# A row maximum over 16384 rows: two stores at the end, a last row in halves, and six rows per partition reduced by TensorE, ScalarE and GpSimd

## The chip, the cores and the metric

The kernel runs on one core of one Trainium2 chip. The metric is the device time of one execution in microseconds (us), given as the median of several runs. Beside the runs there is one execution that the hardware profiler recorded; its durations are the ones used in the working.

## What is computed

```python
def setup_inputs():
    batch, seq, dim = 32, 512, 1024
    return {"x": np.random.randn(batch, seq, dim).astype(np.float32)}

def reference(x):
    return np.max(x, axis=-1).astype(np.float32)
```

The input is 32 x 512 = 16384 rows of 1024 floats (67.1 MB); the output is one float for each row (64 KB). Every input value is read once, so the loads alone are a large part of the time.

## The kernel before

The 16384 rows are cut into two blocks. In a block of S rows per partition, partition p holds S rows that follow one another in memory, so that a load of g rows per partition moves one run of g x 4 KB for each of the 128 partitions. The first block has 112 rows per partition, the second 16. "Row" below always means one row in each of the 128 partitions.

`BLOCKS` (L13 to L16) lists how many rows each load brings: large loads first (14, 14, 12, ...), then smaller ones down to single rows at the end. There are 26 loads. They go into `ring` (L37), a buffer of 46 rows; a load that doesn't fit behind the last one starts again at place 0 (L46, L47), and has to wait until VectorE has reduced the rows that stood there.

For each load there are two statements: SyncE's queue issues the load (L49), and VectorE reduces it to one value a row with one `reduce_max` (L50), which writes into `res`. After each block, ScalarE's queue issues the store of that block's part of `res` (L54). TensorE, ScalarE's arithmetic and GpSimd do nothing, but for four small memsets of the launch (L71).

What sets the order: each engine and each queue takes its instructions in the order of the program. The framework adds the waits: a reduction waits for its load, a load for the reductions that last read its places, a store for the block's reductions. The framework also shares out a few semaphores among all transfers of the SyncE and ScalarE queues in turn, so that a transfer can have to wait for an earlier one to land. L82 is the end of the program.

Of the kernel before, what the change touches and what calls it, by code (L numbers as in the profile page):

```python
# [1 line left out]

# [4 lines left out]


F32 = mybir.dt.float32

BLOCKS = [  # L13
    [14, 14, 12, 11, 9, 8, 8, 7, 6, 5, 4, 4, 4, 3, 3],
    [2, 2, 2, 2, 2, 1, 1, 1, 1, 1, 1],
]  # L16
RING = 46


@with_exitstack  # L20
def kernel(
    ctx: ExitStack,
    tc: tile.TileContext,
    x: bass.AP,
    out: bass.AP,
):
    nc = tc.nc
    P = 128
    X = mybir.AxisListType.X

    xf = x.flatten_outer_dims()
    N, D = xf.shape
    I = N // P
    of = out.flatten_outer_dims()

    once = ctx.enter_context(tc.tile_pool(name="once", bufs=1))
    ring = once.tile([P, RING, D], F32)  # L37
    res = once.tile([P, I], F32)

    at = first = 0  # L40
    for loads in BLOCKS:
        S = sum(loads)
        xb = xf[first * P:(first + S) * P, :].rearrange("(p i) d -> p i d", p=P)
        b = 0
        for g in loads:
            if at + g > RING:  # L46
                at = 0  # L47
            xc = ring[:, at:at + g, :]
            nc.sync.dma_start(out=xc, in_=xb[:, b:b + g, :])  # L49
            nc.vector.reduce_max(out=res[:, first + b:first + b + g], in_=xc, axis=X)  # L50
            at += g
            b += g
        dst = bass.AP(tensor=of.tensor, offset=of.offset + first * P, ap=[[S, P], [1, S]])
        nc.scalar.dma_start(out=dst, in_=res[:, first:first + S])  # L54
        first += S
    assert first == I


# [1 line left out]
_INS = ['x']  # L60
_OUTS = [((32, 512), 'float32')]


# [23 lines left out]
```

## Time and profile before

| | us |
|---|---|
| median of 10 runs | 165.1 (164.98 to 165.37) |
| the profiled execution | 165.25 |
| its span, first to last instruction | 163.5 |
| VectorE busy, 26 reductions | 138.5 |
| VectorE idle, waiting for loads (4 times) | 22.5, of which 20.3 for the first load |
| first load issued | 0.73 |
| first store (56 KB): issued, time to landing | 143.04, 6.6 |
| last reduction: start, duration | 159.82, 1.21 |
| last store (8 KB): issued, time to landing | 161.07, 1.4 |

The profiled execution took 165.25 us, of which 163.5 lie between the first and the last instruction. Times within the profile count from the start of that span. "DVE" in the profile is VectorE, "POOL" is GpSimd, "SPq" is SyncE's queue, "ACTq" ScalarE's. In the row of 40 digits each digit is the busy share of a fortieth of the span in tenths. In the groups of instructions, the columns are: how many, busy time in all, mean nanoseconds of one, idle time before them and what ended it. The chain of waits is followed back from the last instruction: at each step the profile goes to whatever released it last.

### The profile page before, as it was taken

To read this page: it belongs to the slowest core of one execution; us is meant where nothing else is said; L and a number is where in the kernel's file an instruction comes from. 1 tells how busy PE (TensorE), PEld (TensorE's weight loads), DVE (VectorE), ACT (ScalarE), POOL (GpSimd) and SP (SyncE) were. 2 spreads that over 40 slices of the span, in tenths; PEclk is the share of its full clock that TensorE was granted. 3 is DMA by queue.
4 is the path that set the end of the run, shared out by engine and by line. 5 is a ranking of instruction groups with operands and counts; after the bars stand their busy time and mean duration, and the time that the engine had idled before them with its cause. 6 is when DMAs were issued, how large, how long until landed. Compare 5 with 4: busy or idle time off the path is not lost.

```text
span 163.5 us, 109 instructions
## 1 busy us (share of the span) xinstructions
DVE 138.5 (85%) x26; POOL 0.2 (0%) x4
## 2 busy tenths in 40 slices
DVE  0000099968999999999999999999999999999994
POOL 0000000000000000000000000000000000000000
DMA  6999999999899898999999999999999999999980
GB/s 225 449 449 449 449 449 449 449 405 397 385 433 497 353 518 350 433 433 455 441 401 473 409 442 414 427 415 446 410 425 433 429 414 420 419 420 419 411 342 2
DMA packets 4032, 67.18 MB, mean 411 GB/s; under 512 B 704, under 2 KB 704, under 8 KB 1472
## 3 DMA queue, kind: packets, MB, share of 16 engines
q1 hardware_dynamic: 3744, 67.11, 96.3%
q10 hardware_dynamic: 288, 0.07, 0.2%
HBM read 67.11 MB, written 0.07 MB: 411 GB/s over the span
## 4 chain that ended last, share of the span: by engine, by line
DMA 57%; DVE 40%; DVEq 1%; SPq 0%; issue 0%
DMA ring<-in_x_dram 57%; DVE res L50 40%; DVEq L82 1%; SPq L49 0%
## 5 line engine op out<-in xcount | busy, mean ns | idle before, releaser
L50 DVE TENSOR_REDUCE res<-ring 128x1 f32<-128x1024 f32 (+11 forms) x26 | 138.5, 5396 | 22.5 <-DMA ring<-in_x_dram 22.5
L71 POOL MEMSET const-bfloat16-1.0<- 128x1 bf16 x1 | 0.1, 101 | 0.0
L71 POOL MEMSET const-uint8-127<- 128x1 uint8 x1 | 0.1, 101 | 0.0
L71 POOL MEMSET const-float32-0.0<- 128x1 f32 x1 | 0.1, 98 | 0.2 <-issue 0.2
L71 POOL MEMSET const-float32-1.0<- 128x1 f32 x1 | 0.1, 98 | 0.0
## 6 DMA issues: line engine op xcount, KB each, us to landing
ring<-in_x_dram SPq DMA_DIRECT2D x2, 7168.0 KB, 27.8
ring<-in_x_dram SPq DMA_DIRECT2D x2, 4096.0 KB, 31.6
ring<-in_x_dram SPq DMA_DIRECT2D x1, 6144.0 KB, 50.1
ring<-in_x_dram SPq DMA_DIRECT2D x3, 2048.0 KB, 36.7
ring<-in_x_dram SPq DMA_DIRECT2D x1, 5632.0 KB, 29.6
ring<-in_x_dram SPq DMA_DIRECT2D x5, 1024.0 KB, 24.6
ring<-in_x_dram SPq DMA_DIRECT2D x1, 4608.0 KB, 23.6
ring<-in_x_dram SPq DMA_DIRECT2D x1, 3584.0 KB, 38.3
```

What stands on the lines that cost most here:

```text
L50: nc.vector.reduce_max(out=res[:, first + b:first + b + g], in_=xc, axis=X)
L71: nc = _bacc.Bacc("TRN2", target_bir_lowering=False, num_devices=1)
L82: with _tile.TileContext(nc) as tc:
```

## The change

It has three parts that stand in one diff.

First, the stores. Both are issued after all loads. The first block's store gets a dependency of its own on the last reduction of the loop, so that it can't go out earlier.

Second, the last row. Its 1024 values are loaded in two halves. The first half goes to a place in the ring, the second into a small buffer `tail` with 16 places ahead of it. VectorE writes the first half's maximum into the place just ahead of the second half, and then reduces this place and the second half together, which gives the row's maximum.

Third, six rows. Each entry of `BLOCKS` is now (rows loaded, rows of these that VectorE does not reduce, number of the load after whose reduction their results are taken in; loads count from 0). Loads 7 and 9 give away two rows each, loads 10 and 12 one each. Such a row goes through four engines: TensorE turns it in eight pieces of 128x128 into PSUM, so that the 128 partitions lie along the free axis; ScalarE copies the 128x1024 result back; GpSimd takes the maximum over partitions (`partition_all_reduce`); TensorE turns the result back, in eight pieces of one partition, which gives eight partial maxima for each row in PSUM; and VectorE takes the maximum of these eight. `in_turn` ties the instructions of TensorE, and those of VectorE, into the order in which the program names them. A row's turn back is held in a list (`backs`) and put into the program behind the next given-away row's `partition_all_reduce`, or at the next load that gives none away. The identity that TensorE needs is made by GpSimd after the first load has landed.

The load lists change as well: 20 loads in the loop and two halves, in place of 26.

```diff
 BLOCKS = [
-    [14, 14, 12, 11, 9, 8, 8, 7, 6, 5, 4, 4, 4, 3, 3],
-    [2, 2, 2, 2, 2, 1, 1, 1, 1, 1, 1],
+    [(15, 0, -1), (15, 0, -1), (15, 0, -1), (15, 0, -1), (12, 0, -1), (7, 0, -1), (11, 0, -1), (10, 2, 8), (7, 0, -1), (5, 2, 13)],
+    [(4, 1, 15), (2, 0, -1), (2, 1, 18), (1, 0, -1), (1, 0, -1), (1, 0, -1), (1, 0, -1), (1, 0, -1), (1, 0, -1), (1, 0, -1)],
 ]
 RING = 46
...
+    turn = ctx.enter_context(tc.tile_pool(name="turn", bufs=2))
+    allr = ctx.enter_context(tc.tile_pool(name="allr", bufs=2))
+    psum = ctx.enter_context(tc.tile_pool(name="psum", bufs=3, space=bass.MemoryType.PSUM))
+    psmall = ctx.enter_context(tc.tile_pool(name="psmall", bufs=2, space=bass.MemoryType.PSUM))
...
+    PAD = 16
+    tail = once.tile([P, PAD + H], F32)
...
+    def in_turn(engine, inst):
+        if engine in before:
+            tc.add_manual_dep(inst.ins, before[engine].ins.name, NOSYNC, reason="in turn")
+        before[engine] = inst
+        return inst
+
+    def by_gpsimd(rows, cols, m):
+        back = psmall.tile([P, m, C], F32)
+        for k in range(m):
+            ps = psum.tile([P, D], F32)
+            for c in range(C):
+                in_turn("PE", nc.tensor.transpose(
+                    out=ps[:, c * P:(c + 1) * P],
+                    in_=rows[:, k, c * P:(c + 1) * P],
+                    identity=ident,
+                ))
+            sb = turn.tile([P, D], F32)
+            nc.scalar.copy(out=sb, in_=ps)
+            top = allr.tile([P, D], F32)
+            nc.gpsimd.partition_all_reduce(top, sb, P, bass_isa.ReduceOp.max)
+            run(backs)
+
+            def turn_back(top=top, k=k):
+                for c in range(C):
+                    in_turn("PE", nc.tensor.transpose(
+                        out=back[:, k, c:c + 1],
+                        in_=top[0:1, c * P:(c + 1) * P],
+                        identity=ident[0:1, 0:1],
+                    ))
+
+            backs.append(turn_back)
+        return lambda: in_turn("DVE", nc.vector.reduce_max(out=cols, in_=back, axis=X))
+
+    def run(calls):
+        while calls:
+            calls.pop(0)()
...
-            xc = ring[:, at:at + g, :]
-            nc.sync.dma_start(out=xc, in_=xb[:, b:b + g, :])
-            nc.vector.reduce_max(out=res[:, first + b:first + b + g], in_=xc, axis=X)
...
-        nc.scalar.dma_start(out=dst, in_=res[:, first:first + S])
+            xc = ring[:, at:at + n, :]
+            nc.sync.dma_start(out=xc, in_=xb[:, b:b + n, :])
+            cols = res[:, first + b:first + b + n]
+            if m:
+                due.setdefault(w, []).append(by_gpsimd(xc[:, n - m:, :], cols[:, n - m:], m))
+            else:
+                run(backs)
+            if j == 0:
+                nc.gpsimd.tensor_copy(out=ident[:, 0:1], in_=xc[:, 0, 0:1])
+                make_identity(nc, ident)
+            if n > m:
+                reduce = in_turn("DVE", nc.vector.reduce_max(
+                    out=cols[:, :n - m], in_=xc[:, :n - m, :], axis=X))
+            run(due.get(j, []))
...
+    half = ring[:, at, :H]
+    nc.sync.dma_start(out=half, in_=xb[:, b, :H])
+    nc.sync.dma_start(out=tail[:, PAD:], in_=xb[:, b, H:])
+    in_turn("DVE", nc.vector.reduce_max(out=tail[:, PAD - 1:PAD], in_=half, axis=X))
+    in_turn("DVE", nc.vector.reduce_max(out=res[:, I - 1:], in_=tail[:, PAD - 1:], axis=X))
+
+    store = nc.scalar.dma_start(out=views[0][0], in_=views[0][1])
+    tc.add_manual_dep(store.ins, reduce.ins.name, SYNC, reason="behind the loads")
+    nc.scalar.dma_start(out=views[1][0], in_=views[1][1])
```

In it D = 1024, H = D // 2 = 512, C = D // 128 = 8, P = 128, and `ident` is a 128x128 identity; `views` keeps each block's destination and its part of `res`.

## The prediction

> **What bounds the kernel now.** I read the page's busy shares first, then the chain of waits in order of time, then the waits of the load queue, then the groups by shape, then narrow windows at the end.
>
> ```profile
> span 163.5 us, 109 instructions
> DVE 138.5 (85%) x26; POOL 0.2 (0%) x4
> DMA  6999999999899898999999999999999999999980
> ```
>
> The transfers are busy in every slice but the last, and VectorE in 85% of the span. Neither can be called the bound from shares alone: the chain has to say which one is late where.
>
> ```profile
> 1.15 36.06 DMA ring<-in_x_dram
> 37.23 58.01 DVE res L50 x5
> 95.26 36.75 DMA ring<-in_x_dram
> 132.03 19.94 DMA ring<-in_x_dram
> 151.99 7.92 DVE res L50 x6
> 159.91 1.13 DVEq L82
> ```
>
> (Start, duration.) The two alternate. At 95.26 and 151.97 VectorE had caught up and was waiting for a load; in between and after, it was working without a pause. From 151.99 it reduces 8 rows (seven instructions, the timeline gives 9.04) without a wait and ends at 161.03.
>
> ```profile
> SPq L49 <- DVE res L50: 77.6, 7, 15.1
> SPq L49 <- DMA ring<-in_x_dram: 56.6, 10, 18.2
> SPq L49 <- DMA out_dram<-res: 5.0, 1, 5.0
> ```
>
> (Total, times, longest.) The load queue waits a lot, but only for room: the transfers stay busy beneath it. The third line is the first block's store: issued at 143.04, landed 6.6 later at 149.64, and one load of the tail was issued only then (149.7). The loads issued before it were still landing until 157.0, so this wait cost no transfer time.
>
> Issue time plus time to landing gives each load's landing. 14 rows land at 20.3 and 37.2; 12 at 51.8; 11 at 65.0; the last 3-row load at 139.4; the last of the five two-row loads at 151.97; the six singles at about 1.27 apart until 159.6. An n-row load therefore costs about 1.20n + 0.08 (14 rows: 16.9; 4 rows: 4.9; 1 row: 1.27). Checked over the whole: 20.3 + 114 x 1.20 + 25 x 0.08 = 159.1, plus some 0.3 for the store (its queue's 0.2% of the span): 159.4, measured 159.6. So **the loads set the pace**, and VectorE adds a last row and 0.2 of lag behind them.
>
> ```profile
> L50 DVE TENSOR_REDUCE res<-ring 128x14 f32<-128x14336 f32 x2 | 30.2, 15086 | 22.1 <-DMA ring<-in_x_dram 22.1
> L50 DVE TENSOR_REDUCE res<-ring 128x2 f32<-128x2048 f32 x5 | 11.2, 2280 | 0.2 <-DMA ring<-in_x_dram 0.2
> L50 DVE TENSOR_REDUCE res<-ring 128x1 f32<-128x1024 f32 x6 | 6.8, 1208 | 0.0
> ```
>
> The mean ns give VectorE's price: (15086 - 1208) / 13 = 1.068 us a row and about 0.14 an instruction, of which 0.07 shows between instructions that follow directly (9.04 = 8 x 1.068 + 7 x 0.07). VectorE's row is 0.13 cheaper than the loads'; it catches up slowly.
>
> [...]
>
> **The change, part by part.** Loads are numbered 1 to 20 in the new lists, then two halves.
>
> *Store moved.* The first block's store goes from the middle of the tail to behind load 20's reduction. It takes its 0.3 of transfer time out of the load stream, and its queue wait with it. It is put on ScalarE's queue ahead of the last store; issued at about 158.8, 0.38 on the queue, its 56 KB then lands beside the last half row and before the last store is even issued (160.1). Cost 0; if it should land as slowly as before (6.6), the end would be 165.4 instead of 161.5, but that landing was with eight loads queued ahead, which are gone here.
>
> *Load lists.* 22 loads for 26: 4 x 0.08 = 0.3 less. First load 15 rows: 20.3 + 1.2 = 21.5. Then 113 rows x 1.20 + 21 x 0.08: the last half lands at 158.8 (was 159.6). Room in the ring: load 4 needs reduction 1 (21.5 + 16.15 = 37.7) while loads 2 and 3 are queued until 57.7; load 5 needs reduction 2 (55.8), load 6 and 7 reduction 3 (74), loads 8 to 11 reductions 4 and 5 (92, 105), all with more than 15 us of loads ahead of them. Cost 0. GpSimd's rows never gate a load: their places are not used again.
>
> *VectorE.* Load 4 lands at 75.8, and VectorE needs 45 rows until load 8: 75.8 + 48.1 + 4 x 0.07 = 124.1, which is just load 8's landing (124.1). From there it has 32 rows (six fewer than landed), 15 instructions and four small maxima over 8 or 16 values out of PSUM: 34.2 + 1.1 + 4 x 0.15 + 0.1 for the last = 36.0, ending at **160.1**. The small maxima are not in the trace; 0.14 is VectorE's fixed part[...]. The halves: two instructions of 0.61 for one of 1.14; the second can start at 159.4, after its landing at 158.8, so VectorE, not the load, is last, by some 0.7. Without the six rows (6 x 1.07 = 6.4) it would end at 166.5: they are what makes the rest possible.
>
> *The six rows.* For each: eight TensorE transposes F, ScalarE's copy c, GpSimd's maximum A, eight turns back B. None is in the trace.
> [...]
>
> Round trip F + c + A + B = 6.2. TensorE's order is written out by hand, and a row's turn back stands ahead of a later row's transposes: row 5's transposes stand behind row 3's turn back, row 6's behind row 5's. So from load 10's landing (138.65) to row 6's result there are **three whole round trips**, 18.6: 157.2. VectorE reaches the maximum that needs it (after load 19) at 157.5. It fits with 0.3 to spare. The earlier ones: rows 1 and 2 from 124.1 to 133[...], needed at 140.3; row 4 at 148, needed at 151.5; row 5 at 151, needed at 153.9. Behind a late maximum on VectorE stand load 20, both halves and both stores, so lateness goes straight into the end, threefold.
>
> *Setup.* The identity is made on GpSimd after load 1, at 21.5 with 100 us before use: 0. If it delayed the first load instead, all of its time would be seen.
>
> *Sum.* VectorE ends 160.1 for 161.03: -0.9. The store and closing stay 2.45 (163.5 - 161.03). Profiled execution: 165.25 (span 163.5 and 1.75 around it) -> 164.3. The median of the runs, 165.1, lies 0.15 under it: **164.2**.
>
> **Rivals.**
> - *The gain is eaten* (same): load 8 lands 0.4 later, as the measured excess of 0.2 and single-row spacing of up to 1.4 allow, and the small maxima take 0.25 with their waits: 160.1 + 0.4 + 0.4 = 160.9, so 165.0. For it: VectorE is the later of the two over the whole last 36 us, with no wait left to swallow anything. Against: the loads are fewer.
> - *The round trip is too long* (slower): its place is VectorE's wait for row 6, after load 19. It decides from 3 x (round trip) > 18.85 + 0.9 + 0.3, a round trip of 6.7. At 7.5 row 6 comes at 161.15, 3.65 late, and the time is 164.15 + 3.65 = 167.8.[...] For it: only 0.5 separates my estimate from it, and four terms are unseen. Against: no profile row[...].
>
> **How the numbers follow.** A difference of 0.2% (0.33 us) is about what a measurement of this kernel can tell from none. Forecast 0.57 (own range 163.6 to 164.7), eaten 0.10, too long 0.33. About half of the last lies below 167.8 (a round trip of 7.5). The range 163.6 to 167.8 leaves out the rest of it, some 0.17, and 0.02 below.
>
> **What would show it.** Right: VectorE's busy time near 134 (122 x 1.068 + 22 x 0.14 + 0.6); no wait of VectorE for TensorE over 0.3; the last load landing near 158.8; VectorE's end near 160.1. GpSimd's mean of one near 2.9 and the eight transposes within 1.4. Wrong: VectorE waiting for TensorE after load 19 (too long), a late first store, or POOL work ahead of the first load.

## The result and the profile after

| | before | after |
|---|---|---|
| median of the runs, us | 165.11 (28 runs) | 169.09 (8 runs, 168.29 to 170.21) |
| profiled execution | 165.25 | 168.57 |
| its span | 163.5 | 166.6 |
| time around the span | 1.75 | 1.97 |
| VectorE's last reduction ends | 161.03 | 164.32 |

The changed kernel is slower: ratio 1.0241, 95% interval 1.0224 to 1.0258. The forecast was 164.2 and faster. The rival "the round trip is too long" had the sign and the place; its own number, 167.8, was still 1.3 short.

As in the prediction, loads are counted from 1 here. Of the six rows that VectorE gives away, 1 and 2 come with load 8, 3 and 4 with load 10, 5 with load 11 and 6 with load 13.

The page of the changed kernel, in the order in which the kernel before was read: busy shares, then the shares of the chain.

```profile
span 166.6 us, 329 instructions
PE 16.5 (10%) x96; PEld 14.7 (9%) x96; DVE 132.7 (80%) x26; ACT 7.4 (4%) x7; POOL 20.2 (12%) x13
DMA 56%; DVE 29%; POOL 4%; PE 4%; issue 3%; POOLq 2%; ACT 1%; SPq 0%; ACTq 0%
```

VectorE does 5.8 us less than before, as the six rows promise, and none of the new engines is busy for more than 12%. Shares of busy time would call this a good trade. But POOL, PE and ACT have appeared in the chain. Who waited for whom (total, times, longest):

```profile
DVE res L124 <- DMA ring<-in_x_dram: 28.0, 5, 21.3
DVE res L95 <- PE back L88: 3.5, 1, 3.5
POOL ident masks.py:199 <- issue: 10.0, 1, 10.0
```

L95 is VectorE's maximum over the turned-back values, L88 the turn back. One wait of 3.5 us, where I had worked out 0.3 to spare; the 10.0 of GpSimd comes back below. The chain of waits of the changed kernel shows what it waited for (start, duration, what):

```profile
139.46 1.99 PE ps L75 x8
...
141.53 1.02 ACT sb L81
142.55 0.08 issue
142.63 3.23 POOL top L83
145.86 0.04 issue
145.91 1.01 PE back L88 x8
146.92 1.92 PE ps L75 x8
...
150.01 3.22 POOL top L83
153.24 4.11 issue
157.34 3.28 POOLq L168
160.63 0.04 issue
160.67 1.02 PE back L88 x8
161.69 0.02 issue
161.71 0.04 DVE res L95
161.75 0.04 issue
161.80 1.21 DVE res L124
163.01 0.60 DVE tail L136
163.61 0.02 issue
163.63 0.69 DVE res L137
```

Read it from the top: load 10 has landed; turn, copy, maximum and turn back of row 3; then the turn of row 5 right behind that turn back at 146.92; and so on. The "issue" of 4.11 hides row 5's turn back and row 6's turn and copy, and "POOLq L168" is row 6's maximum. The timeline of TensorE has the turns in full, with row 5's turn back just ahead of row 6's transposes.

```profile
145.91 1.01 PE L88 MATMUL back<-ident,top 1*128 1x1 f32 x8 [3.13 <-POOL top L83]
146.85 1.97 PE L75 MATMUL ps<-ident,ring 128*128 128x128 f32 x8
149.12 1.01 PE L88 MATMUL back<-ident,top 1*128 1x1 f32 x8 [0.30 <-POOL top L83]
153.29 1.01 PE L88 MATMUL back<-ident,top 1*128 1x1 f32 x8 [3.17 <-POOL top L83]
154.23 1.97 PE L75 MATMUL ps<-ident,ring 128*128 128x128 f32 x8
160.67 1.01 PE L88 MATMUL back<-ident,top 1*128 1x1 f32 x8 [4.47 <-POOL top L83]
```

Row 6's data landed at 149.3, and TensorE was free between 150.13 and 153.29. It stood still for 3.17 us in front of row 5's turn back, which waited for GpSimd, while the transposes behind it were ready. From 139.46 to 161.69 there are three round trips of 7.4: 22.2 us instead of the 18.6 of the prediction.

The second difference lies much earlier. Load 8 landed at 124.8 instead of 124.1, because load 2 came 18.6 us after load 1, where 18.1 had been worked out. VectorE, which has no slack from there on, asks for row 6 at 158.2 instead of 157.5.

### The profile page after: what moved, and what is told of

Its sections match the earlier page's. It is cut to its first block, busy times and chain, and to the rows that moved or that the text cites. A ratio compares the mean times of both kernels' runs of the same rounds, so it can differ in the third digit from the quotient of the medians.

```text
span 166.6 us, 329 instructions
## 1 busy us (share of the span) xinstructions
PE 16.5 (10%) x96; PEld 14.7 (9%) x96; DVE 132.7 (80%) x26; ACT 7.4 (4%) x7; POOL 20.2 (12%) x13
## 3 DMA queue, kind: packets, MB, share of 16 engines
q1 hardware_dynamic: 3168, 67.11, 94.4%
HBM read 67.11 MB, written 0.07 MB: 403 GB/s over the span
## 4 chain that ended last, share of the span: by engine, by line
DMA 56%; DVE 29%; POOL 4%; PE 4%; issue 3%; POOLq 2%; ACT 1%; SPq 0%; ACTq 0%
DMA ring<-in_x_dram 56%; DVE res L124 28%; POOL top L83 4%; PE ps L75 2%; POOLq L168 2%; ACT sb L81 1%; PE back L88 1%; DVE res L137 0%; DVE tail L136 0%; SPq L113 0%; DVE res L95 0%; ACTq L81 0%
## 5 line engine op out<-in xcount | busy, mean ns | idle before, releaser
L124 DVE TENSOR_REDUCE res<-ring 128x1 f32<-128x1024 f32 (+7 forms) x20 | 131.3, 6600 | 28.1 <-DMA ring<-in_x_dram 28.0
L83 POOL PARTITION_ALL_REDUCE top<-sb x6 | 19.4, 3256 | 109.2 <-ACT sb L81 109.2
L75 PE MATMUL ps<-ident,ring 128*128 128x128 f32 x48 | 10.9, 415 | 128.8 <-DMA ring<-in_x_dram 128.8
L75 PEld LDWEIGHTS ps<-ident,ring 128*128 128x128 f32 x48 | 9.5, 222 | 128.9 <-issue 124.9
L81 ACT COPY sb<-ps 128x1024 f32<-128x1024 f32 x6 | 6.1, 1012 | 149.2 <-PE ps L75 149.2
L88 PE MATMUL back<-ident,top 1*128 1x1 f32 x48 | 5.7, 235 | 16.4 <-POOL top L83 16.4
L88 PEld LDWEIGHTS back<-ident,top 1*128 1x128 f32 x48 | 5.2, 201 | 18.0 <-POOL top L83 18.0
L95 DVE TENSOR_REDUCE res<-back 128x2 f32<-128x16 f32 (+1 forms) x4 | 0.7, 162 | 3.5 <-PE back L88 3.5
L137 DVE TENSOR_REDUCE res<-tail 128x1 f32<-128x513 f32 x1 | 0.7, 687 | 0.0
L136 DVE TENSOR_REDUCE tail<-ring 128x1 f32<-128x512 f32 x1 | 0.7, 676 | 0.0
## 6 DMA issues: line engine op xcount, KB each, us to landing
ring<-in_x_dram SPq DMA_DIRECT2D x1, 5120.0 KB, 32.3
```

What stands on the lines that cost most here:

```text
L75: in_turn("PE", nc.tensor.transpose(out=ps[:, c * P:(c + 1) * P], in_=rows[:, k, c * P:(c + 1) * P], identity=ident,))
L81: nc.scalar.copy(out=sb, in_=ps)
L83: nc.gpsimd.partition_all_reduce(top, sb, P, bass_isa.ReduceOp.max)
L88: in_turn("PE", nc.tensor.transpose(out=back[:, k, c:c + 1], in_=top[0:1, c * P:(c + 1) * P], identity=ident[0:1, 0:1],))
L95: return lambda: in_turn("DVE", nc.vector.reduce_max(out=cols, in_=back, axis=X))
L124: reduce = in_turn("DVE", nc.vector.reduce_max(out=cols[:, :n - m], in_=xc[:, :n - m, :], axis=X))
```

## The experiments

Two theories stand after this. **Round trips:** three of them in a row, tied together by TensorE's written order, each longer than estimated, put row 6 late. **Late loads:** something around 20 to 40 us delays load 2, in some executions load 3 as well, by 0.4 to 1.2 us together, and the whole kernel with them. Rivals of the first: GpSimd's four maxima in a row are the limit; the use of GpSimd costs time by itself. Rival of the second: longer loads are slower.

### The first step of the change alone

Edit: the load lists of before, no row given away; both stores at the end, last row in halves.

> The load lists of before (the last single row in two halves), both stores at the end, no row given away. If the loss of the change sits only in the six rows, as the round-trip theory says, this part alone should be a little faster than before: the store's 0.3 us leaves the load stream (last landing 159.3 for 159.6) and the last reduction shrinks from 1.21 to about 0.7, so 0.5 to 0.8 us faster, 164.3 to 164.6. If the stores' move or the halves cost something, it is at or over 165.1.

Measured: 165.24 against 165.09, ratio 1.0009 (1.0001 to 1.0017). The promised 0.5 to 0.8 isn't there; the kernel is 0.15 slower, and the interval only just leaves out no difference. In the end of its chain the two halves run directly behind the singles:

```profile
151.72 7.74 DVE res L120 x6
159.46 0.10 issue
159.56 0.69 DVE tail L132
160.25 0.02 issue
160.27 0.69 DVE res L133
```

VectorE, not the load, is last. A last load in halves can't help there: it makes two instructions (0.69 + 0.69 and the small waits) out of one of 1.21. To tell the halves from the store, the store was moved alone (`held` is the last reduction but one; the diff is against the kernel before):

```diff
-        nc.scalar.dma_start(out=dst, in_=res[:, first:first + S])   # behind each block
+    store = nc.scalar.dma_start(out=views[0][0], in_=views[0][1])   # behind all loads
+    tc.add_manual_dep(store.ins, held.ins.name, SYNC, reason="behind the loads")
```

> The kernel before with nothing changed but the first block's store, which now waits for the last reduction but one. The prediction had it take 0.3 us out of the load stream: 164.8. e1_stores_halves (165.2, with the halves) saw a last landing only 0.1 to 0.2 earlier, so the other reading is: the 56 KB cost the loads 0.1 at most, and with the last row whole, 164.9 to 165.1.

Measured: 165.00 against 165.11, ratio 0.9992 (0.9986 to 0.9998). The last load landed 139.2 us after the first (159.2 and 20.0; before: 139.3). The store had cost the loads 0.1, not 0.3; its landing took only 1.6 us at the end. So the store gives 0.1 and the halves take 0.2 to 0.3 in this setting.

### TensorE's order: one turn back later

```diff
             else:
-                run(backs)
+            elif j != 11:
+                run(backs)
```

(`j` counts from 0, so this is load 12 by the counting of the text.) Load 12 no longer puts row 5's turn back into the program; it comes behind row 6's transposes.

> The changed kernel with one line different: the turn back of row 5 stays behind row 6's transposes on TensorE. Round-trip theory: row 6's transposes then start at about 150.1 instead of 154.2, GpSimd takes rows 5 and 6 back to back (153.2 to 156.5), row 6's result is there at 157.6, before VectorE asks for it at 158.2; the 3.5 us wait is gone and VectorE ends near 160.8, so 3.5 us faster than the changed kernel: about 165.0 by the profile beside it. If GpSimd's own time is the limit, or if the loss lies outside the wait, it stays above 167.

Measured: 165.83 (ratio 1.0046, 1.0027 to 1.0065), 3.3 us under the changed kernel. VectorE has no wait for TensorE left. GpSimd takes rows 5 and 6 0.55 apart (lines of the timeline of this kernel):

```profile
149.94 3.22 POOL L83 PARTITION_ALL_REDUCE top<-sb  x1 [0.39 <-ACT sb L81]
153.71 3.22 POOL L83 PARTITION_ALL_REDUCE top<-sb  x1 [0.55 <-ACT sb L81]
156.99 1.01 PE L88 MATMUL back<-ident,top 1*128 1x1 f32 x8 [2.77 <-POOL top L83]
158.64 0.15 DVE L95 TENSOR_REDUCE res<-back 128x1 f32<-128x8 f32 x1
```

Row 6 is back at 158.0, before VectorE asks for it at 158.64. GpSimd itself was not the limit. The time isn't 165.0 but 165.8, though VectorE's end, 161.30, is near the 160.8 expected: the late loads were 0.5 later still here, and the time around the span was 2.4 in this execution.

### Two rows fewer

```diff
-    [(4, 1, 15), (2, 0, -1), (2, 1, 18), (1, 0, -1), ...
+    [(4, 0, -1), (2, 0, -1), (2, 0, -1), (1, 0, -1), ...
```

> The changed kernel with rows 5 and 6 given back to VectorE (four rows through GpSimd, none after load 9). Round-trip theory: the wait is gone, VectorE has 2 x 1.07 us more and two small maxima of 0.15 less: it ends at 164.3 - 3.5 + 2.1 - 0.3 = 162.6, so about 1.7 us faster than the changed kernel and 1.8 slower than before (166.9). If using GpSimd at all costs time outside VectorE's path, the distance between VectorE's end and the device time is larger than the 4.2 us of before.

Measured: 166.88 (1.011, 1.0096 to 1.0125); VectorE ends at 162.57, 162.6 expected, without a wait for TensorE. The distance from VectorE's end to the device time is 166.62 - 162.57 = 4.05 (before: 4.22), so no hidden price of using GpSimd shows here. Giving the two rows back costs VectorE 2 us of work and still beats the changed kernel by 2.2.

### How many round trips count

```diff
+            mid = once.tile([P, D], F32)
-            nc.scalar.copy(out=sb, in_=ps)
+            nc.scalar.copy(out=mid, in_=ps)
+            nc.scalar.copy(out=sb, in_=mid)
```

The changed kernel, with each row's copy made in two steps.

> The changed kernel with ScalarE's copy made twice (PSUM to a buffer, buffer to the GpSimd input), which adds 1.0 to 1.2 us to each row's round trip and nothing to TensorE or GpSimd. Theory of three round trips in a row: row 6 comes 3 x 1.1 = 3.3 us later, 172.4. If GpSimd's four maxima in a row set row 6 (two round trips and four maxima), 2.2 us later, 171.3. If only row 6's own latency counts, 1.1 us, 170.2.

Measured: 172.23 (1.0438, 1.0418 to 1.0459), 3.1 over the changed kernel. In the profile, row 6's maximum on GpSimd and then on VectorE:

```profile
161.21 3.22 POOL L85 PARTITION_ALL_REDUCE top<-sb  x1 [5.29 <-ACT sb L83]
165.54 0.17 DVE L97 TENSOR_REDUCE res<-back 128x1 f32<-128x8 f32 x1 [4.97 <-PE back L90]
```

VectorE's part starts 3.83 later than in the changed kernel (161.71); 0.43 of this is load 10, whose transposes start at 139.89 for 139.46. The rest, 3.40, is three times 1.13: the second copy's 1.04 and its handover. Two trips (2.3) or one (1.1) are excluded. The prediction's "threefold" holds.

### Does GpSimd cost time by itself?

```diff
+            if first == 0 and b == 0:
+                nc.gpsimd.tensor_copy(out=src, in_=xc[:, 0, :])
+                nc.gpsimd.partition_all_reduce(top, src, P, bass_isa.ReduceOp.max)
```

> The kernel before with one GpSimd copy and one partition maximum of 128x1024 behind the first load, whose result nobody uses (the output is that of before). It is off every path, so the round-trip theory expects 165.1 plus nothing. The rival[...] expects 0.2 to 1 us more, either as a later landing of the loads around 20 to 40 us (in the changed kernel load 2 came 18.6 us after load 1, where 18.1 was worked out) or outside the span (time less span was 1.75 before and 2.0 to 2.9 in the runs of the changed kernel).

Measured: 165.22 against 165.09 (1.0006, 0.9998 to 1.0014): nothing that can be told from none. Then the same with an identity made as in the change:

```diff
+                make_identity(nc, ident)
```

> The kernel before with the same idle GpSimd work as e4_one_maximum and the making of an identity between the copy and the maximum[...]; its result is used by nobody. [...] loads 2 and 3 land 0.5 to 1 us later than in e4_one_maximum (37.0 and 51.6), and as the loads set the pace, the end moves by as much: 165.6 to 166.2. If the late loads of the changed kernel come from the longer load list or from TensorE's and ScalarE's use, 165.2 as in e4_one_maximum.

Measured: 166.12 (1.0059, 1.0047 to 1.0072): **1.0 us** for work that nobody waits for, on an engine that was idle. The trace has a pair of instructions MODIFY_POOL_CONFIG ahead of the selection (at 0.9) and ahead of the maximum (at 21.5), and behind each pair idle time that nothing releases, 10.43 and 10.11 us:

```profile
0.72 0.20 POOL masks.py:197 MEMSET ident<- 128x128 f32 x1 [0.30 <-POOLq L81]
11.36 0.28 POOL masks.py:199 TENSOR_SCALAR_AFFINE_SELECT ident<-ident 128x128 f32<-128x128 f32 x1 [10.43 <-issue]
20.29 1.04 POOL L58 COPY src<-ring 128x1024 f32<-128x1024 f32 x1 [8.64 <-DMA ring<-in_x_dram]
31.43 3.24 POOL L60 PARTITION_ALL_REDUCE top<-src  x1 [10.11 <-issue]
```

Load 2 lands at 37.6 (37.0 with the maximum alone), load 3 at 52.2 (51.6), the last at 160.1 (159.5). So this execution, at 165.85 the fastest of the five, shows 0.6 of the 1.0. Beside the second idle stretch, from 21.3 to 31.4, load 2 took 0.5 longer. Beside the first, from 0.9 to 11.4, load 1 was not delayed (20.2 against 20.1); why the loads lose time beside one and not beside the other stays open. The changed kernel has the same two pairs, at 21.8 ahead of the selection, with 10.0 us of idle time behind it, and at 32.3 ahead of the maximum, whose first input comes only at 128.

### A maximum ahead of the identity

If the order of the two makes the idle time and the late loads, selection first and maximum behind it, then a small maximum ahead of the identity may spare both:

```diff
                 nc.gpsimd.tensor_copy(out=ident[:, 0:1], in_=xc[:, 0, 0:1])
+                nc.gpsimd.partition_all_reduce(ident[:, 16:17], ident[:, 0:1], P, bass_isa.ReduceOp.max)
                 make_identity(nc, ident)
```

On top of the later turn back:

> The kernel with the later turn back (e2_turn_back_later), and one 128x1 partition maximum ahead of the identity[...]. [...] GpSimd's idle 11 us ahead of the identity is gone, loads 2 to 4 come 18.1 apart, load 8 lands near 124.2 instead of 125.3, VectorE ends near 160.6 instead of 161.3: 0.6 to 1.0 us faster than e2_turn_back_later, 164.9 to 165.2. If the late loads have another cause, 165.8 as there.

Measured: **164.45**, ratio 0.9967 (0.9954 to 0.9979): faster than both kernels, by 0.6 than the one before. GpSimd's idle 11 us (11.1 in the kernel with the later turn back) are gone in its timeline: the same selection runs without a wait behind the maximum (the memset ends at 22.22, the selection starts at 22.30), so it is the order of the two that costs. Why it does is not shown.

```profile
21.61 0.35 POOL L122 PARTITION_ALL_REDUCE ident<-ident  x1
22.02 0.20 POOL masks.py:197 MEMSET ident<- 128x128 f32 x1
22.30 0.29 POOL masks.py:199 TENSOR_SCALAR_AFFINE_SELECT ident<-ident 128x128 f32<-128x128 f32 x1
```

Loads 2 to 4 each come 18.1 to 18.2 behind the load before (18.7 and 18.8 for loads 2 and 3 with the later turn back alone), though they bring as many rows as in the change, so their length isn't what made them late. Load 8 lands at 124.1, the last half at 158.9, and VectorE ends at 160.16.

And alone, with TensorE's order as in the change:

> [...] TensorE's order as in the change. Both theories together: the loads come 0.6 to 1.1 us earlier, and load 10 with them, so row 6's result comes as much earlier and the wait of 3.5 us stays; about 168.3 (169.1 less 0.6 to 1.1). If the late loads had made the wait, it would fall well under 3 us, and the time under 167.

Measured: 167.91 (1.0175, 1.016 to 1.0189). VectorE's wait for row 6 is 3.5, as in the changed kernel, only earlier. With this the square is full, in medians:

| | selection first | small maximum first |
|---|---|---|
| turn back as in the change | 169.09 | 167.91 |
| turn back later | 165.83 | 164.45 |

TensorE's order is worth 3.3 and 3.5, the small maximum 1.2 and 1.4: within what these medians can tell, the two causes add.

### Two further looks

The last row whole, in the best kernel:

> The kernel with both repairs (e5_one_library), its last row whole instead of in halves. In e5 VectorE takes the halves at 158.84 and 159.47 and ends at 160.16, with the last half landed at 158.9. Whole, the row would land at about 158.8 and be reduced from 158.9 to 160.1: the same within 0.1, so 164.4 to 164.6. If the halves do save what the half-length last reduction promises (0.5 us), this kernel is at 164.9 or more.

Measured: 164.64 (0.997, 0.9963 to 0.9977), the same as with halves (0.9967). VectorE reduces load 20 until the last row lands (159.0) and ends at 160.24, with halves at 160.16: the halves do nothing here.

The time around the span, with 32 idle transposes added to the kernel with four rows:

> The kernel with four rows (e3_four_rows) and 32 more transposes of the identity behind its making, early and off every path, so that TensorE has as many instructions (96 transposes) as in the changed kernel. Question: the runs of the changed kernel and of e2_turn_back_later lie 2.0 to 3.0 us over their spans, those of before and of e3_four_rows 1.75 to 1.85. If the number of TensorE's instructions makes that, the distance grows to 2.0 to 3.0 here and the median from 166.9 to about 167.4; if not, 166.9 and 1.8.

Measured: 166.93 (1.0105, 1.0089 to 1.012), against 166.88 without them; three of its four runs lie 1.74 to 1.81 over their spans and one 2.56. The number of TensorE's instructions doesn't make it. The runs of the kernel before and of the two that use GpSimd alone lie 1.7 to 1.85 over their spans; runs of kernels that use TensorE lie 1.75 to 3.0 over them, from run to run. Which part of TensorE's use does this, and where, stays open.

## Why the prediction was wrong

**What held.** VectorE's busy time (134 forecast, 132.7). The load formula, 1.20n + 0.08, with which the last half was to land at 158.8 and load 8 at 124.1: with the small maximum ahead of the identity they land at 158.9 and 124.1. VectorE's end without a wait, 160.1: measured 160.16 in the kernel with both repairs, whose time is 164.45 where 164.2 was forecast. That three whole round trips lie between load 10 and row 6: shown by the doubled copy. The place, VectorE's wait after load 19, named as what would show it wrong.

**The step that failed** is "Round trip F + c + A + B = 6.2 ... 18.6: 157.2 ... It fits with 0.3 to spare." The path was right, three trips in a row; the size of one trip was not: it took 7.4. The 6.2 was my estimate, and so were the 1.4 for F and the 2.9 for A that the prediction names as signs; no trace of the kernel before has any of the four terms. The terms A and c by their groups in the changed kernel (mean ns after the busy time); F and B are in TensorE's timeline above:

```profile
L83 POOL PARTITION_ALL_REDUCE top<-sb x6 | 19.4, 3256 | 109.2 <-ACT sb L81 109.2
L81 ACT COPY sb<-ps 128x1024 f32<-128x1024 f32 x6 | 6.1, 1012 | 149.2 <-PE ps L75 149.2
```

- F: 1.97 for 1.4, the largest error.
- A: 3.23 for 2.9.
- c and B: 1.01 each, 2.0 for the 1.9 that the 6.2 leaves for the two.
- Handovers between the engines, four or five of 0.02 to 0.08: 0.2 for 0.

Together 7.4 for 6.2, so 22.2 for 18.6. The path takes the sum three times and had a slack of 0.3; 1.2 too little in one trip became 3.6.

Behind F and B stands one thing that the prediction had no term for: TensorE goes at two paces in these traces. The kernel with the idle transposes has both in one unbroken burst; the changed kernel has a fast turn back at 131.35:

```profile
32.86 1.97 PE L126 MATMUL ps<-ident 128*128 128x128 f32 x8 [32.86 <-POOL ident masks.py:199]
37.21 1.25 PE L126 MATMUL ps<-ident 128*128 128x128 f32 x10
131.35 0.66 PE L88 MATMUL back<-ident,top 1*128 1x1 f32 x8 [2.78 <-POOL top L83]
```

At the slow pace a turn's pieces start 213 ns apart and eight take 1.97; at the fast pace they start 109 ns apart, ten take 1.25 and eight, by these starts, 1.04. A turn back takes 1.01 or 0.66. Every turn and turn back of rows 3, 5 and 6 on the three trips ran at the slow pace (1.97 and 1.01). The granted clock is 0.50 in both windows below, of which the first has the turn back of row 2, the second row 5's turn back and row 6's turn:

```profile
132.00:136.00 4.00, 1.02 (x9) 0.93 (x8) 4.00 (x2) 0.00 (x0) 2.53 (x1) 0.50 1.02 435
152.00:156.00 4.00, 2.71 (x16) 2.49 (x16) 3.94 (x7) 0.00 (x0) 1.24 (x1) 0.50 1.03 410
```

(Columns: stretch, its length, busy time and count of PE, PEld, DVE, ACT and POOL, TensorE's granted clock, DMA share, GB/s.)

Over the fast turn back, from 131.3 to 132.0, the clock is 1.00. The column has to be read with care: from 126.7 to 128.6 it says 1.00 too, although the pieces of row 2 start the slow pace's 213 ns apart there. The durations tell the pace.

An estimate from these figures, which no run tried: at the fast pace a trip would be 1.04 + 1.01 + 3.23 + 0.66 + 0.2 = 6.1 and three of them 18.4; from 139.46 row 6 would be back at 157.9, ahead of VectorE's 158.2. So the sum of 6.2 lay near a fast trip partly by luck: its 1.4 for F is 0.4 above a fast turn, its 2.9 for A 0.3 below the measured maximum. The slow pace alone is worth 1.3 in a trip. What decides on the pace is not shown here; in the burst above it changed between 34.83 and 37.21.

**The second step** is "The identity is made on GpSimd after load 1 ... with 100 us before use: 0." The 100 us were there, but the cost was not GpSimd's time. It was the loads': 0.5 to 1 us, where the selection stood ahead of the first maximum. The traces show 10.0 to 11.7 us of idle time on GpSimd ahead of the selection, and loads 2 and 3 that land later beside it or behind it; the prediction had no price for late loads. How the one delays the other is not shown: the page of the changed kernel lists the loads' 67.11 MB, the stores' 0.07 and no other transfer.

**Smaller.** The store's 0.3 in the load stream was 0.1. The halves were priced at 1.22 for the pair and measured 1.4 (the second waits for the first's result). The rest of the miss, in the profiled execution: VectorE's end 4.2 later than forecast (3.5 of wait, 0.7 of late loads), 0.2 less behind it, 0.2 more around the span: 168.6 for 164.3. The median lies 0.5 over this execution, where 0.15 under it had been assumed: the eight runs lie 2.0 to 2.9 over their spans, which stays open.

**On the chances.** The rival held 0.33, with half of it beyond 7.5 for the trip. The range's upper end sat at that number. The trip stayed 0.1 under it, but the late loads (0.8 at load 10) and the larger distance from span to time, which the rival did not have, took the time past 167.8. Errors of unseen terms need not cancel: F and B hang on the same pace, and it took both up at once (1.97 for 1.04, 1.01 for 0.66).

## What to carry to other kernels

When work goes around through several engines, write down which instruction of the next round stands behind which result of the last one. TensorE took its instructions in the written order here, and stood still for 3.17 us ahead of one "turn back" with ready work behind it: one that is written early makes rounds that could overlap run one after the other, and multiplies every error in the price of a round. Ask of each step at what pace its engine will run there, not only what it costs at its best; here the pace was worth 1.3 us a round. Put work that is ready ahead of work that waits; here a single moved group of instructions was worth 3.3 us. And an engine's idle time does not make what it does free: here work that nobody waited for cost 1.0 us. Look at what else was in flight then.

## What was not expected of the hardware

- GpSimd's selection, where it stood ahead of the first maximum, came with 10.0 to 11.7 us of idle time that nothing releases; in the load-bound kernel, with two such idle times in the execution, selection and maximum cost 1.0 us; the maximum alone cost 0.13, with an interval that includes none.
- A partition maximum of 128x1024 floats takes 3.23 us, one of 128x1 0.35. VectorE's 8-row reduction beside it took 8.69, as before (8.68): the maximum did not slow it.
- TensorE ran at the slower of two paces on all three trips: eight 128x128 turns took 1.97 us there and take 1.04 by the 109 ns of the fast pace; eight turns back took 1.01 and 0.66.
- Device times of kernels that use TensorE lay 1.75 to 3.0 us over their spans, those of the others 1.7 to 1.85; unexplained.
